# A two-layer hybrid transformer on one core: the norm's shift moves from a row addition to feature columns where transposes leave PSUM, modulation starts two pairs later, the last tile is finished by halves

## The chip, the cores and the metric

The kernel runs on one core of a Trainium2 chip. The metric is the device time of one execution in microseconds (us), as the median of several runs; less is better. A core has TensorE for matrix products and transposes (PE in the profile; PEld is its loading of weights), VectorE (DVE), ScalarE (ACT), GpSimd (POOL) and SyncE (SP), whose queue issues all data transfers of this kernel. Each engine takes its instructions in the order of its own queue. Data is computed on in SBUF, 128 partitions wide; products arrive in PSUM; the inputs and large intermediates lie in device memory.

## The reference

All is in float32: 1024 tokens, 1024 features, two layers. A condition vector gives each layer six rows of 1024 numbers, the modulation: shift, scale and gate for the mixer, shift, scale and gate for the MLP.

```
cond = silu(c)
for l in range(2):
    mod = (cond @ w_ada[l] + b_ada[l])[:, None, :]
    sh_m, sc_m, g_m, sh_f, sc_f, g_f = jnp.split(mod, 6, axis=-1)
    h = _rmsnorm(x, norm_g[l, 0]) * (1.0 + sc_m) + sh_m
    y = _hybrid_mixer(h, ...)        # attention, latent attention, state space model, output projection
    x = x + g_m * _rmsnorm(y, norm_g[l, 1])
    h = _rmsnorm(x, norm_g[l, 2]) * (1.0 + sc_f) + sh_f
    y = jnp.square(jax.nn.relu(h @ w_up[l])) @ w_down[l]
    x = x + g_f * _rmsnorm(y, norm_g[l, 3])
```

The change concerns the lines that make `h`: a norm over the features of a token, a product with a row, and the addition of a shift row.

## The kernel before, in words

**Tiles.** The tokens are eight tiles of 128, the features eight blocks of 128. The norm works token by token, so tokens lie on partitions and features along the row. The products that read `h` want features on partitions. So each normalised tile is transposed on PE into PSUM, block by block, and cut there into two parts, high and low: ACT rounds the value (`nc.scalar.copy`, L611 and L619) and DVE stores what the rounding left (L612 and L620). A product of two such numbers is three matmuls (`mm3`, L192 to L194).

**The norm** (`norm`, L595): ACT squares a tile and sums along the row (L599), `rstd` makes the reciprocal root with one ACT and four DVE instructions (L183 to L187), DVE multiplies by the root and the scale row in one pass (L600), and POOL adds the shift row (L601). Both rows lie in SBUF as 128 equal copies of 1024 numbers, loaded by `mod_load` (L591). In the last two tiles of the layer border the addition is made by DVE (`NVEC`, L1473).

**Where norms run.** Three places use them:

- At the end of each mixer, `renorm` (L1271) takes tiles 0 to 3 beside the output projection of tiles 6 and 7 (L1313), and transposes each by `transp8` with `wide=True` (one PSUM tile of 1024).
- Tiles 4 to 7 follow as `late` while the MLP's first products already run (`mlp_up`, L329 to L333). The up projection uses a scheme that saves products: for each pair `i` of feature blocks, `plain(i)` needs only tiles 0 to 3, and `sums(i)` needs sums and differences of tiles 0 to 3 with 4 to 7. `transp_late` (L201) makes these operands: POOL adds high and low part of tile t-4 (L208), PE transposes tile t, and four differences (L217) are each cut in high and low (L230, L231). Six `plain` stages lead (`LEAD`). Weights come as 512 or 1024 KB loads (L265), POOL forms their sums (L273 to L279), and ACT and DVE cut them.
- At the border of the layers, the last group of the down projection calls `finish(t)` per token tile (L1460). It adds the tile's result to the residual (`Net.finish`, L622: square L628, multiplication L629, addition on POOL L630, store L631), normalises tile t-1 for the next layer, and transposes tile t-3 by narrow steps of four blocks. Tiles 4 to 7 are transposed in `late_norm`, beside the next layer's first projections.

**Modulation.** The rows of the next stages are computed beside the MLP by `mod_stream`, in chunks of 128 columns (`mod_chunk`): a step loads a chunk's weights, bias and gain; the next runs eight multiply-adds on DVE (L540); the third sums over partitions with two small PE products (L551 and L553, both within `bank_t`), adds or multiplies, and stores 128 numbers. In layer 0 there are 56 chunks: two steps after each of 16 pairs in `mlp_up`, the others in `mlp_down`, one after a token tile. In layer 1 there is nothing left to do.

**Order and memory.** The program is written in one order; `TileContext(nc, schedule_with_timeline_sim=True)` sets the order of each engine's queue from a simulated timeline, with the program's order as priority. Row tiles, weights and intermediates share one arena of 17856 words a partition (`Arena`); a block that is given back is used again, and the new user waits for the old one's last reader.

## Time and profile before

| | |
|---|---|
| median of 3 runs | 2843.18 us (2840.31 to 2851.27) |
| the profiled execution | 2845.56 us, its span 2843.7 us |
| mean granted clock of TensorE | 0.955 |
| DMA | 313.10 MB, 110 GB/s on average |

The span goes from the first to the last instruction. A row of the profile names the line of the program, the engine, the operation, what it writes and reads, and its shape; "x24: 1276/1285/3091" is a count with the least, median and greatest duration in ns. In a timeline, a row is start (us), duration, engine, line, operation, and in brackets how long the engine was idle before it and what ended that. In a table of waits, a row is who waited for whom, us in total, times, and the longest. `arena_f` is the arena, `split` the space for high and low parts, `bank_...` a PSUM tile. Where the page breaks the span into 40 slices, the granted clock of PE is:

```
PEclk9899989899989999999989998899998999999999
```

### The profile page before, as it was taken

To read this page: it belongs to the slowest core of one execution; us is meant where nothing else is said; L and a number is where in the kernel's file an instruction comes from. 1 tells how busy PE (TensorE), PEld (TensorE's weight loads), DVE (VectorE), ACT (ScalarE), POOL (GpSimd) and SP (SyncE) were. 2 spreads that over 40 slices of the span, in tenths; PEclk is the share of its full clock that TensorE was granted. 3 is DMA by queue.
4 is the path that set the end of the run, shared out by engine and by line. 5 is a ranking of instruction groups with operands and counts; after the bars stand their busy time and mean duration, and the time that the engine had idled before them with its cause. 6 is when DMAs were issued, how large, how long until landed. Compare 5 with 4: busy or idle time off the path is not lost.

```text
span 2843.7 us, 34676 instructions
## 1 busy us (share of the span) xinstructions
PE 2642.4 (93%) x12530; PEld 2063.0 (73%) x12530; DVE 1734.4 (61%) x3163; ACT 1109.0 (39%) x2129; POOL 641.2 (23%) x533
## 2 busy tenths in 40 slices
PE   5799999898879999999979999989987999999997
PEld 4677776676657777777768777767766888778886
DVE  7767666644878787565463575765458555533435
ACT  5243444544534455121142443445445455621112
POOL 1441233210433320000042113342014433000002
PEclk9899989899989999999989998899998999999999
DMA  6441212313355457443140131132134333531303
GB/s 224 115 136 53 91 51 83 97 62 110 115 162 163 152 175 239 131 149 119 67 138 32 56 93 47 57 112 87 52 111 123 129 112 115 190 125 67 119 30 119
DMA packets 265551, 313.10 MB, mean 110 GB/s; under 512 B 25570, under 2 KB 209060, under 8 KB 265380
## 3 DMA queue, kind: packets, MB, share of 16 engines
q1 hardware_dynamic: 265380, 310.88, 34.1%
q8 instruction: 99, 1.62, 0.2%
q14 instruction: 72, 0.59, 0.1%
HBM read 244.41 MB, written 66.43 MB: 109 GB/s over the span
## 4 chain that ended last, share of the span: by engine, by line
PE 66%; DVE 8%; DMA 6%; issue 4%; ACT 3%; POOL 2%; SPq 0%; POOLq 0%; DVEq 0%; ACTq 0%
PE bank_b L192 10%; PE bank_b L194 10%; PE bank_b L193 10%; PE bank_s L192 8%; PE bank_s L193 8%; PE bank_s L194 8%; PE bank_a L843 2%; PE bank_s L896 2%; DVE split L231 2%; PE bank_t L856 2%; DMA arena_f<-in_w_up 1%; DVE arena_f L540 1%; DMA d_r<-arena_f 1%; PE bank_a L872 1%; PE bank_b L1189 1%
## 5 line engine op out<-in xcount | busy, mean ns | idle before, releaser
L192 PE MATMUL bank_b<-split 128*128 128x512 f32 (+2 forms) x1824 | 727.4, 399 | 36.1 <-ACT split L230 15.5
L193 PE MATMUL bank_b<-split 128*128 128x512 f32 (+2 forms) x1824 | 709.9, 389 | 2.3 <-DVE split L612 1.9
L194 PE MATMUL bank_b<-split 128*128 128x512 f32 (+2 forms) x1824 | 708.1, 389 | 1.6 <-DVE split L231 1.2
L230 ACT CAST split<-arena_f 128x512 fp32r<-128x512 f32 (+1 forms) x384 | 282.9, 761 | 693.5 <-PE bank_s L193 432.9
L192 PE MATMUL bank_s<-split 128*128 128x512 f32 (+2 forms) x1152 | 454.3, 397 | 17.4 <-ACT arena_f L376 7.0
L193 PE MATMUL bank_s<-split 128*128 128x512 f32 (+2 forms) x1152 | 450.4, 391 | 9.2 <-DVE split L231 6.5
L194 PE MATMUL bank_s<-split 128*128 128x512 f32 (+2 forms) x1152 | 447.6, 389 | 0.0
L192 PEld LDWEIGHTS bank_b<-split 128*128 128x128 f32 x1824 | 353.1, 194 | 119.3 <-issue 17.4
L231 DVE TENSOR_TENSOR split<-arena_f,split 128x512 fp32r<-128x512 f32 (+1 forms) x384 | 358.1, 950 | 97.7 <-ACT split L230 96.1
L194 PEld LDWEIGHTS bank_b<-split 128*128 128x128 f32 x1824 | 352.7, 193 | 70.9 <-issue 2.5
L193 PEld LDWEIGHTS bank_b<-split 128*128 128x128 f32 x1824 | 353.8, 194 | 67.2 <-issue 4.7
L378 DVE TENSOR_TENSOR arena_f<-arena_f,bank_s 128x1024 f32<-128x1024 f32 x128 | 156.1, 1219 | 263.1 <-PE bank_s L194 263.1
L192 PEld LDWEIGHTS bank_s<-split 128*128 128x128 f32 (+1 forms) x1152 | 217.7, 190 | 73.2 <-ACT arena_f L376 8.8
L193 PEld LDWEIGHTS bank_s<-split 128*128 128x128 f32 (+1 forms) x1152 | 218.8, 190 | 56.6 <-DVE split L231 9.0
L194 PEld LDWEIGHTS bank_s<-split 128*128 128x128 f32 (+1 forms) x1152 | 218.6, 190 | 43.8 <-issue 1.0
L831 ACT ACTIVATE arena_f<-bank_s,nm 128x128 f32<-128x128 f32 (+3 forms) x192 | 141.9, 741 | 182.7 <-DVE nm L830 151.3
L830 DVE TENSOR_REDUCE nm<-bank_s 128x1 f32<-128x128 f32 (+3 forms) x192 | 142.0, 752 | 113.4 <-PE bank_s L898 58.0
L540 DVE SCALAR_TENSOR_TENSOR arena_f<-arena_f,cond 128x128 f32<-128x128 f32 x448 | 164.5, 396 | 56.4 <-DMA arena_f<-in_b_ada 27.2
L630 POOL TENSOR_TENSOR arena_f<-arena_f 128x1024 f32<-128x1024 f32 x16 | 39.5, 2470 | 479.6 <-DVE arena_f L629 473.7
L246 ACT ACTIVATE arena_f<-arena_f 128x512 f32<-128x512 f32 x128 | 80.8, 632 | 137.0 <-DVE arena_f L320 61.6
L896 PE MATMUL bank_s<-split 32*128 32x512 f32 (+3 forms) x576 | 120.8, 384 | 12.3 <-ACT arena_f L831 10.0
L859 ACT COPY arena_f<-bank_t 128x512 f32<-128x512 f32 (+1 forms) x160 | 86.8, 542 | 105.6 <-PE bank_t L856 91.8
(276 smaller groups left out, 3266.3 us busy)
## 6 DMA issues: line engine op xcount, KB each, us to landing
arena_f<-in_w_ada SPq DMA_DIRECT2D x80, 512.0 KB
d_r<-arena_f SPq DMA_DIRECT2D x128, 256.0 KB
arena_f<-in_w_up SPq DMA_DIRECT2D x32, 1024.0 KB
arena_f<-d_r SPq DMA_DIRECT2D x64, 512.0 KB
arena_f<-in_w_down SPq DMA_DIRECT2D x64, 512.0 KB
arena_f<-d_x SPq DMA_DIRECT2D x36, 512.0 KB
d_x<-arena_f SPq DMA_DIRECT2D x24, 512.0 KB
arena_f<-in_w_in SPq DMA_DIRECT2D x20, 512.0 KB
```

Source lines behind the costliest of these rows:

```text
L192: mm(out, wh, xh, start=start, stop=False)
L193: mm(out, wh, xl, start=False, stop=False)
L194: mm(out, wl, xh, start=False, stop=stop)
L230: self.nc.scalar.copy(hi, src)
L231: (eng or self.nc.vector).tensor_sub(lo, src, f32(hi))
L246: nc.scalar.activation(t, t, AF.Relu)
L378: nc.vector.tensor_add(y[t], y[t], ps)
L540: nc.vector.scalar_tensor_tensor(acc, in0=w[:, k], scalar=self.cond[:, k:k + 1], in1=acc, op0=ALU.mult, op1=ALU.add)
L830: nc.vector.tensor_reduce(nm, S[:, 0:n], axis=AX.X, op=ALU.max, negate=True)
L831: nc.scalar.activation(p[:, 0:n], S[:, 0:n], AF.Exp, bias=nm, accum_out=ls)
L859: nc.scalar.copy(held, ps[:, 0:w])
L896: nc.tensor.matmul(S[mp][:, c0:c1], Q[rw, a, tok], K[rw, b, c0:c1], start=a == b, stop=a == 1 and c1 < n)
```

## The change

The shift is no longer added as a row. `mod_cols` loads it as eight columns, one number per feature, 8 words a partition instead of 1024: element (p, k) comes from address 128 k + p. `norm` ends with the multiplication. `cut_cols` adds the shift while the transposed tile is read from PSUM, feature block by feature block: ACT makes the high part with the column as bias, DVE the low part as (value + column) - high, so a wide tile takes eight instructions on each engine in place of one. In `transp_late` the first two differences take the column in four pieces each, and the high and low part of blocks 4 to 7 are cut by `cut_cols`. The late tiles' operands on POOL (L208) stay.

The modulation of `mlp_up` begins after the third pair (28 steps there in place of 32), and four more steps run in the last but one group of `mlp_down`.

The last token tile of each layer's MLP is finished by halves of 512 features: DVE adds the first half of the product as soon as it is complete, ACT squares the two halves apart, a small DVE instruction adds the two sums, and the multiplication, the addition of the residual (by DVE, not POOL) and the store are made for each half.

At the border the two loaded vectors are given back after the last transposition, not before the first.

```diff
--- before.py
+++ after.py
@@ -29,7 +29,6 @@
 OFF = 0, 0, 0.1, 2
 OUTS = (), (0, 1), (2, 3), (4, 5)
 WOW = 16
-NVEC = 6
 GROUPS = [2] + [4] * 6 + [2, 4]
 LEAD = 6
 C_Q, C_K, C_V, C_CQ, C_CKV, C_KR, C_Z, C_XBC, C_DT = 0, 256, 512, 768, 1024, 1152, 1184, 1696, 2464
@@ -198,7 +197,7 @@
 
         return [self.slot(2 * n, 2, 4, 512) for n in range(4)]
 
-    def transp_late(self, x, hT, t):
+    def transp_late(self, x, hT, t, shift):
 
         nc, F = self.nc, self.F
         T = self.sums()
@@ -211,17 +210,22 @@
             nc.tensor.transpose(ps[:, k * P:k * P + P], x[:, k * P:k * P + P], self.ident)
         pv = ps.rearrange("p (n k q) -> p n k q", n=2, q=P)
 
-        def put(n, a, c):
+        def put(n, a, c, b=None):
 
             e = F.get(4, P)
-            nc.vector.tensor_sub(e, a, c)
+            if b is None:
+                nc.vector.tensor_sub(e, a, c)
+            else:
+                for k in range(4):
+                    nc.vector.scalar_tensor_tensor(e[:, k], in0=a[:, k], scalar=b[:, k:k + 1], in1=c[:, k],
+                                                   op0=ALU.add, op1=ALU.subtract)
             self.split(e, *(T[n][:, m, :, sl] for m in range(2)))
             return e
 
-        e1 = put(0, pv[:, 0], b[0])
-        e2 = put(1, pv[:, 1], e1)
+        e1 = put(0, pv[:, 0], b[0], shift[:, 0:4])
+        e2 = put(1, pv[:, 1], e1, shift[:, 4:8])
+        self.cut_cols(pv[:, 1], shift[:, 4:8], *(h[:, 4:8, tok] for h in hT))
         e3 = put(2, e2, b[0])
-        self.split(pv[:, 1], *(h[:, 4:8, tok] for h in hT))
         e4 = put(3, b[1], e2)
         F.put(e1, e2, e3, e4, *b)
 
@@ -335,8 +339,9 @@
             if i >= LEAD:
                 plain(i)
             sums(i)
-            next(bg, None)
-            next(bg, None)
+            if i > 1:
+                next(bg, None)
+                next(bg, None)
 
     def mlp_down(self, l, y, bg, finish):
 
@@ -367,14 +372,17 @@
             for t in range(NT):
                 tok = slice(t * P, t * P + P)
                 ps = self.bank2()
+                tip = last and t == NT - 1
                 for dh in range(2):
                     dd = slice(dh * 512, dh * 512 + 512)
                     for n, ((_, r), (_, wd)) in enumerate(rw):
                         self.mm3(ps[:, dd], r[:, 0, tok], r[:, 1, tok], wd[:, 0, dd], wd[:, 1, dd], n == 0, n == size - 1)
+                    if tip:
+                        nc.vector.tensor_add(y[t][:, dd], y[t][:, dd], ps[:, dd])
                 if g == 0:
                     y.append(F.get(D, top=True))
                     nc.scalar.copy(y[t], ps)
-                else:
+                elif not tip:
                     nc.vector.tensor_add(y[t], y[t], ps)
                 if last:
                     finish(t)
@@ -591,16 +599,29 @@
         self.nc.sync.dma_start(t, self.d_mod[l, sec:sec + 1].to_broadcast([P, D]))
         return t
 
-
-    def norm(self, x, a, b, xn, eng=None):
+    def mod_cols(self, l, sec):
+
+        t = self.F.get(KD)
+        self.nc.sync.dma_start(t, self.d_mod[l, sec].rearrange("(k p) -> p k", p=P))
+        return t
+
+
+    def norm(self, x, a, xn):
 
         nc = self.nc
         ss = self.sm(1, "nss")
         nc.scalar.activation(xn, x, AF.Square, accum_out=ss)
         nc.vector.scalar_tensor_tensor(xn, in0=x, scalar=self.rstd(ss), in1=a, op0=ALU.mult, op1=ALU.mult)
-        (eng or nc.gpsimd).tensor_add(xn, xn, b)
-
-    def transp8(self, x, hi, lo, t, wide=False):
+
+    def cut_cols(self, ps, b, hi, lo):
+
+        nc = self.nc
+        for k in range(ps.shape[1]):
+            nc.scalar.activation(hi[:, k], ps[:, k], AF.Identity, bias=b[:, k:k + 1])
+            nc.vector.scalar_tensor_tensor(lo[:, k], in0=ps[:, k], scalar=b[:, k:k + 1], in1=f32(hi[:, k]),
+                                           op0=ALU.add, op1=ALU.subtract)
+
+    def transp8(self, x, hi, lo, t, wide=False, b=None):
         nc = self.nc
         sl = slice(t * P, t * P + P)
         if wide:
@@ -608,6 +629,9 @@
             for k in range(KD):
                 nc.tensor.transpose(ps[:, k * P:k * P + P], x[:, k * P:k * P + P], self.ident)
             pv = ps.rearrange("p (k q) -> p k q", q=P)
+            if b is not None:
+                self.cut_cols(pv, b, hi[:, :, sl], lo[:, :, sl])
+                return
             nc.scalar.copy(hi[:, :, sl], pv)
             nc.vector.tensor_sub(lo[:, :, sl], pv, f32(hi[:, :, sl]))
             return
@@ -616,8 +640,7 @@
             for k in range(4):
                 nc.tensor.transpose(ps[:, k * P:k * P + P], x[:, (k0 + k) * P:(k0 + k) * P + P], self.ident)
             pv = ps.rearrange("p (k q) -> p k q", q=P)
-            nc.scalar.copy(hi[:, k0:k0 + 4, sl], pv)
-            nc.vector.tensor_sub(lo[:, k0:k0 + 4, sl], pv, f32(hi[:, k0:k0 + 4, sl]))
+            self.cut_cols(pv, b[:, k0:k0 + 4], hi[:, k0:k0 + 4, sl], lo[:, k0:k0 + 4, sl])
 
     def finish(self, y, src, g, dst, t, x, u, junk):
 
@@ -625,6 +648,21 @@
         tok = slice(t * P, t * P + P)
         nc.sync.dma_start(x, src[tok])
         ss = self.sm(1, "fss")
+        if t == NT - 1:
+
+            s2 = self.sm(2, "fss")
+            for h in range(2):
+                dd = slice(h * 512, h * 512 + 512)
+                nc.scalar.activation(junk[:, h * 4:h * 4 + 4], y[:, dd].rearrange("p (k q) -> p k q", q=P), AF.Square,
+                                     accum_out=s2[:, h:h + 1])
+            nc.vector.tensor_scalar(ss, s2[:, 0:1], s2[:, 1:2], None, op0=ALU.add)
+            rs = self.rstd(ss)
+            for h in range(2):
+                dd = slice(h * 512, h * 512 + 512)
+                nc.vector.scalar_tensor_tensor(u[:, dd], in0=y[:, dd], scalar=rs, in1=g[:, dd], op0=ALU.mult, op1=ALU.mult)
+                nc.vector.tensor_add(x[:, dd], x[:, dd], u[:, dd])
+                nc.sync.dma_start(dst[tok, dd], x[:, dd])
+            return
         nc.scalar.activation(junk, y.rearrange("p (k q) -> p k q", q=P), AF.Square, accum_out=ss)
         nc.vector.scalar_tensor_tensor(u, in0=y, scalar=self.rstd(ss), in1=g, op0=ALU.mult, op1=ALU.mult)
         nc.gpsimd.tensor_add(x, x, u)
@@ -1277,13 +1315,13 @@
         else:
             x = F.get(D)
             self.nc.sync.dma_start(x, src[t * P:t * P + P])
-        self.norm(x, *nxt, u)
+        self.norm(x, nxt[0], u)
         F.put(x)
         yield 1.0
         if t < 4:
-            self.transp8(u, hT[0], hT[1], t, True)
+            self.transp8(u, hT[0], hT[1], t, True, nxt[1])
         else:
-            self.transp_late(u, hT, t)
+            self.transp_late(u, hT, t, nxt[1])
         F.put(u)
         yield 1.0
 
@@ -1308,7 +1346,7 @@
             self.weave((1.0, self.chain(*(out(t, cTs[t % 2]) for t in OUTS[i])), OFF[i]),
                        ((4 + i * 16 + 20) / 11.5 / len(OUTS[i]), self.until(m, i)))
         self.drain(m)
-        nxt = self.mod_load(l, 4), self.mod_load(l, 3)
+        nxt = self.mod_load(l, 4), self.mod_cols(l, 3)
         kept = {}
         self.weave((26, self.chain(out(6, own(6), kept), out(7, own(7), kept))),
                    (9, self.chain(*(self.renorm(t, dst, nxt, hT) for t in range(4)))))
@@ -1462,15 +1500,15 @@
                     tail["g"] = self.mod_load(l, 5)
                     tail["x"] = [F.get(D) for _ in range(3)]
                     if more:
-                        tail["nxt"] = (self.mod_load(l + 1, 1), self.mod_load(l + 1, 0))
+                        tail["nxt"] = (self.mod_load(l + 1, 1), self.mod_cols(l + 1, 0))
                         tail["w"] = list(self.stage_w(I["w_in"][l + 1], self.qk_cols(0), 2))
                 if more and t == NT - 1:
                     tail["w0"] = self.load_w(tail["w"], 2)
                 if more and 2 < t < 7:
-                    self.transp8(y[t - 3], hT[0], hT[1], t - 3)
+                    self.transp8(y[t - 3], hT[0], hT[1], t - 3, False, tail["nxt"][1])
                     F.put(y[t - 3])
                 if more and 0 < t <= NT:
-                    self.norm(tail["x"][(t - 1) % 3], *tail["nxt"], y[t - 1], nc.vector if t > NVEC else nc.gpsimd)
+                    self.norm(tail["x"][(t - 1) % 3], tail["nxt"][0], y[t - 1])
                 if t < NT:
                     self.finish(y[t], self.d_x[2 * l], tail["g"], o, t, tail["x"][t % 3], y[t],
                                 hT[0][:, :, t * P:t * P + P])
@@ -1487,11 +1525,11 @@
                 F.put(tail["g"])
                 if more:
                     finish(NT)
-                    F.put(*tail["nxt"])
                     for t in range(4, NT):
-                        self.transp8(y[t], hT[0], hT[1], t, True)
+                        self.transp8(y[t], hT[0], hT[1], t, True, tail["nxt"][1])
                         F.put(y[t])
                         yield
+                    F.put(*tail["nxt"])
                 else:
                     F.put(*y)
                 F.put(*tail["x"])
```

## Prediction

> **What bounds the kernel now.** I read the page first, then three tables by stage, then the waits of PE in the same stages. The page gives the span and the busiest engine:
>
> ```profile
> span 2843.7 us, 34676 instructions
> PE 2642.4 (93%) x12530; PEld 2063.0 (73%) x12530; DVE 1734.4 (61%) x3163; ACT 1109.0 (39%) x2129; POOL 641.2 (23%) x533
> ```
>
> PE is busy for all but 201 us, so only an edit that lets PE start earlier counts. The change touches four places: the late tiles beside the first products of the MLP in layer 0 and in layer 1, the border between the layers, and the very end. The first three (columns: stretch, its length, busy time of each engine, granted clock, DMA share, GB/s):
>
> ```profile
> 720.00:830.00 110.00, 85.01 (x362) 66.50 (x363) 90.79 (x163) 50.59 (x92) 42.39 (x27) 0.89 0.45 136
> 2120.00:2230.00 110.00, 92.85 (x405) 74.06 (x404) 85.28 (x129) 56.52 (x102) 53.62 (x32) 0.92 0.39 122
> 1465.00:1540.00 75.00, 53.64 (x273) 45.27 (x272) 43.27 (x75) 26.25 (x47) 30.28 (x12) 0.80 0.25 80
> ```
>
> PE lacks 25.0 us in the first, 17.2 in the second, 21.4 in the third: a third of all its idle time in a tenth of the span. What it waited for there, in the same order (two rows for the first, one for the second, two for the third):
>
> ```profile
> PE bank_t L551 <- DVE arena_f L540: 12.7, 1, 12.7
> PE bank_t L551 <- DVE arena_f L559: 3.0, 2, 2.6
> PE bank_b L192 <- ACT split L230: 11.4, 3, 6.7
> PE bank_t L617 <- POOL arena_f L601: 14.1, 1, 14.1
> PE bank_s L609 <- DVE arena_f L601: 6.0, 1, 6.0
> ```
>
> L551 and L540 belong to the modulation, L601 is the addition of the shift row, L230 cuts weights into high and low part. So two of the three edits name the releaser of a long wait of PE.
>
> **Border of the layers: the shift leaves the norm.** Two tiles running, on POOL and on DVE:
>
> ```profile
> 1490.93 3.36 POOL L601 TENSOR_TENSOR arena_f<-arena_f 128x1024 f32<-128x1024 f32 x1 [4.03 <-DVE arena_f L600]
> 1494.26 2.39 POOL L630 TENSOR_TENSOR arena_f<-arena_f 128x1024 f32<-128x1024 f32 x1
> 1500.48 3.38 POOL L601 TENSOR_TENSOR arena_f<-arena_f 128x1024 f32<-128x1024 f32 x1 [3.84 <-DVE arena_f L600]
> ```
>
> ```profile
> 1499.11 1.29 DVE L600 SCALAR_TENSOR_TENSOR arena_f<-arena_f,rstd_y 128x1024 f32<-128x1024 f32 x1
> 1500.32 1.28 DVE L629 SCALAR_TENSOR_TENSOR arena_f<-arena_f,rstd_y 128x1024 f32<-128x1024 f32 x1
> ```
>
> This is a ring with a period of 9.55 us (1490.93 to 1500.48). L630, the residual of tile t, stands on POOL's queue behind L601 of tile t-1; the norm of tile t waits for L630; its L600 stands in front of L629 of tile t+1. Without L601 the round is L630's start to L600's (1494.26 to 1499.11, 4.85), L600 and L629 at 1.21 from start to start, so 7.3 us: 2.25 less for each of tiles 4 to 7, and tile 7 also loses its own L601 on DVE. About 10 us of advance stands against PE's second wait of 6.0. The first wait loses tile 3's own addition, 3.3, and pays about 0.5 for small pieces (priced below): 2.8. That brings PE to tile 7 2.8 earlier, so the ring needs 8.8 in all, and has 10. I take 2.8 + 6.0 = 8.8. PE's clock in this stretch is 0.80: 53.64 x 0.20 = 10.7 us lost behind its two long waits; with one of them gone I credit 2, well under half. Border: **10.8**, from 5 (only tile 3 and one round) to 16 (the first wait shrinks too, because the stretched DVE pieces around it get shorter).
>
> **Modulation two pairs later.** In layer 0, tile 7's operands and the first weights of the sums share DVE with modulation steps, and POOL waits for them too:
>
> ```profile
> 782.43 0.39 PE L194 MATMUL bank_b<-split 128*128 128x512 f32 x1
> 800.17 0.80 PE L192 MATMUL bank_b<-split 128*128 128x512 f32 x1
> ```
>
> ```profile
> 782.62 2.78 DVE L540 SCALAR_TENSOR_TENSOR arena_f<-arena_f,cond 128x128 f32<-128x128 f32 x3 [2.32 <-DMA arena_f<-in_w_ada]
> 792.63 2.81 DVE L540 SCALAR_TENSOR_TENSOR arena_f<-arena_f,cond 128x128 f32<-128x128 f32 x8
> ```
>
> ```profile
> 796.25 1.26 POOL L273 TENSOR_TENSOR arena_f<-arena_f 128x512 f32<-128x512 f32 x1 [11.10 <-DVE arena_f L540]
> ```
>
> Between its last plain product and its first product on sums PE waits and runs modulation products, nothing else: 17.7 us from start to start. Without modulation there, tile 7's four differences follow its transposes directly, without L540 in front of them and between them, and L273 doesn't wait for the block that L540 gives back. Read directly, PE would resume some 2.7 us after 782.8, and 14.7 would be won. Layer 1 is the other bound: it has no modulation in this place, and PE still lacks 17.2 us there, for weights whose loads come late; the difference of the two stretches is 7.8. I take **10**, nearer to layer 1, since its stretch is the same code without the work that moves.
>
> A step that moves takes along its loads of weights, bias and gain and its store on SP, eight L540 on DVE, a memset on POOL, two products on PE. Four of them land behind the last ones of this stage, in the product of the down projection:
>
> ```profile
> L540 DVE SCALAR_TENSOR_TENSOR arena_f<-arena_f,cond x200: 329/347/354, 1099.8 to 1336.6; 128x128 f32<-128x128 f32 x100
> 1340.00:1400.00 60.00, 58.52 (x256) 46.80 (x256) 20.81 (x20) 6.00 (x6) 0.00 (x0) 1.00 0.15 45
> ```
>
> 4 x 8 x 0.347 = 11 us of DVE go where it has 39 of 60 idle, and DMA is at 0.15. I put that at 0; if these steps slid into the last eight tiles, which PE passes in half the time, it would cost up to 4.
>
> **Small pieces where transposes leave PSUM.** Eight additions of one feature block each replace one instruction of 1024. Neither engine shows just this form; the nearest rows are the 128x128 forms with a per-row operand on ACT and from PSUM on DVE:
>
> ```profile
> L831 ACT ACTIVATE arena_f<-bank_s,nm 128x128 f32<-128x128 f32 x24 | 8.7, 368 | 17.4 <-DVE nm L830 16.8 <-PE bank_b L1207 0.6
> L611 ACT CAST split<-bank_s 128x1024 fp32r<-128x1024 f32 x28 | 28.3, 1015 | 22.2 <-PE bank_s L609 22.0
> L874 DVE TENSOR_TENSOR arena_f<-bank_a,ml_rl 128x128 f32<-128x128 f32 x32 | 9.2, 288 | 36.6 <-PE bank_a L872 24.2 <-ACT arena_f L1255 7.7 <-ACT arena_f L831 3.5
> L612 DVE TENSOR_TENSOR split<-bank_s,split 128x1024 fp32r<-128x1024 f32 x28 | 34.1, 1222 | 17.1 <-ACT split L611 16.7
> L217 DVE TENSOR_TENSOR arena_f<-bank_s,arena_f 128x512 f32<-128x512 f32 x16 | 11.0, 686 | 1.3 <-POOL arena_f L208 1.0
> ```
>
> A wide tile costs DVE 8 x 0.288 - 1.222 = 1.08 more and ACT 8 x 0.368 - 1.015 = 1.93 more; ACT is busy 51 of 110 us in the late stretch, which covers it. The latency from transposes to the last piece is at most 8 x 0.368 + 0.288 = 3.2 instead of 2.24. A late tile has eight pieces for two L217 (+0.93) and four for one more 128x512 form (4 x 0.288 - 0.686 = +0.47): 1.40 on DVE. A narrow tile pays 8 x 0.288 - 2 x 0.686 = 0.93. Twelve wide, eight late and four narrow tiles: 13.0 + 11.2 + 3.7 = 28 us of DVE in all. [...] What comes back:
>
> ```profile
> L601 POOL TENSOR_TENSOR arena_f<-arena_f 128x1024 f32<-128x1024 f32 x22 | 62.3, 2836 | 166.7 <-DVE arena_f L600 148.2 <-ACT arena_f L859 12.5 <-issue 3.2
> L600 DVE SCALAR_TENSOR_TENSOR arena_f<-arena_f,rstd_y 128x1024 f32<-128x1024 f32 x24 | 38.8, 1625 | 1.7 <-DMA arena_f<-d_mod 1.2
> L600 DVE SCALAR_TENSOR_TENSOR arena_f<-arena_f,rstd_y x24: 1276/1285/3091, 697.4 to 2180.7; 128x1024 f32<-128x1024 f32 x24
> L540 DVE SCALAR_TENSOR_TENSOR arena_f<-arena_f,cond x24: 341/352/1234, 776.8 to 795.1; 128x128 f32<-128x128 f32 x24
> ```
>
> Each tile is transposed 2.84 us earlier, less at most 1 for the small pieces. And L600, in itself 1.28, takes up to 3.09 while POOL adds beside it; its mean is 1.62, so 24 x 0.34 = 8 us come back on DVE from this line alone. In layer 0 the late stretch also gives away L540, of which it had 24 ahead of 800 (8 us by the median), against 4 x 1.40. Each DVE piece waits for ACT's piece of the same block, which runs one ahead; behind it on DVE stand the next tile's norm and the low parts of weights, and PE behind those, which is why DVE's load is a rival below. In the two late stretches I therefore take a small gain, **1.5 each**, from -3 to +3: what is late next there are the loads of w_up, which no edit hurries, except that the shift takes 8 words for each row instead of 1024 and leaves a block for one more load.
>
> The shift's new load, in the place of the second L591, has 1024 pieces of four bytes:
>
> ```profile
> q1 hardware_dynamic: 265380, 310.88, 34.1%
> 689.91 1.58 SPq L591 DMA_DIRECT2D arena_f<-d_mod  x2
> 703.24 1.01 ACT L611 CAST split<-bank_s 128x1024 fp32r<-128x1024 f32 x1 [0.38 <-PE bank_s L609]
> ```
>
> 0.341 x 16 x 2843.7 / 265380 makes 58 ns a packet, so 64 on each of 16 engines are an estimated 3.7 us; its first reader, which takes the place of this L611, comes 12 us behind the issue. I cost it at 0, and up to 3 if a packet of four bytes takes several times as long.
>
> **Last tile by halves.**
>
> ```profile
> 2832.68 1.22 DVE L378 TENSOR_TENSOR arena_f<-arena_f,bank_s 128x1024 f32<-128x1024 f32 x1 [0.63 <-PE bank_s L194]
> 2833.93 1.06 ACT L628 ACTIVATE split<-arena_f 128x1024 fp32r<-128x1024 f32 x1 [3.96 <-DVE arena_f L378]
> 2835.11 0.29 ACT L183 ACTIVATE rstd_y<-fss,eps 128x1 f32<-128x1 f32 x1
> 2836.20 1.28 DVE L629 SCALAR_TENSOR_TENSOR arena_f<-arena_f,rstd_y 128x1024 f32<-128x1024 f32 x1
> 2837.56 2.34 POOL L630 TENSOR_TENSOR arena_f<-arena_f 128x1024 f32<-128x1024 f32 x1 [3.03 <-DVE arena_f L629]
> ```
>
> From L378 to the end of L630 are 7.2 us. After: half the addition (0.69), half the square (the whole took 2833.93 to 2835.11 with its readout; half 0.8), one small sum (0.2), the same 1.1 from L183 to L629, and four half instructions on DVE at 0.62 from start to start (2.5): 5.3. The first half's store is under way by then. **2.3**, from 1.5 to 3.
>
> Sum: 10.8 + 10 + 3 + 2.3 = 26.1 us. The profiled execution took 2845.56 (span and 1.9 around it), so 2819.5; it stood 2.4 above the median of the runs shown, 2843.18, so **2817**.
>
> **Rivals.** *Weights take the place of the wait.* L230 with 11.4 us in layer 1 speaks for it, that layer 0's loads are issued by the same queue too. Then the modulation gives 7.8, the small pieces cost 1.4 x 4 in each late stretch, the border gives 8.8 and the end 2.3: 7.7 in all, 2835.5. *The queues don't follow the program.* The order on each engine comes from a simulated schedule; L551 stands on PE's queue ahead of the sums' products that precede it in the program. If the steps are pulled forward again, the 10 and the two 1.5 fall away: 13 us, 2830. Against it: two pairs are 144 products, 33 us of PE's work at the 58.52 us for 256 above. *DVE becomes the bound.* If POOL's additions were hidden anyway and the 28 us of small pieces lay on the path, less the 8 given back and 2.3 at the end, the time would be 2861. This decides from the point where DVE's busy time in the late stretch comes near its length; it is 91 and 85 of 110 now, and each addition of L601 has PE or DVE waiting behind it at the border, which speaks against.
>
> **How the numbers follow.** About 0.5%, 14 us, can be told from no change. Forecast 0.66, weights 0.16, queues 0.08, DVE 0.10. The forecast's own range is 2802 (border 16, modulation 14.7, late stretches 6, end 3, clock 1) to 2829. The two middle rivals fall within 0.5% (0.24). The range reaches to 2837 to take these in, and leaves out the slower rival and half of what lies around its ends.
>
> **What would show it.** After: no wait of PE on L601's successor of more than a few us past tile 3 at the border, and POOL's L630 some 7 us apart; the gap before the first product on sums in layer 0 under 10 us, with no modulation product in it; the last store's issue about 5 us behind the last L378 half. I am wrong if that gap stays at 17, if PE waits for the small pieces of L611's and L612's successors by more than 10 us in all, or if the waits for L230 grow by what the modulation gave up.

## The result, and the profile after

The changed kernel takes 2820.14 us (median of 4 runs, 2814.24 to 2823.98) against 2846.68 for the kernel before beside it. The ratio is 0.9906, 95% interval 0.9877 to 0.9936: faster, by more than the 0.5% that can be told from no change. Measured again later beside other kernels it was 0.9931 (0.9906 to 0.9956). The forecast, 2817.0 of 2843.18, is a ratio of 0.9908.

The page of the profiled execution after (2822.46 us):

```profile
span 2820.4 us, 34988 instructions
PE 2621.0 (93%) x12530; PEld 2048.1 (73%) x12530; DVE 1747.9 (62%) x3351; ACT 1134.2 (40%) x2265; POOL 576.7 (20%) x509
```

PE does the same 12530 products in 23.3 us less. It lacks 199.4 us of the span, against 201.3: PE waits hardly less, its products became shorter (2642.4 to 2621.0 busy). The granted clock, 0.955 and now 0.958, explains a part of that: the clock lost over the span (its length times one minus the clock) falls from about 128 to 118 us. So the first view says already that the mechanism is not quite the one forecast. The tables by stage, moved to where the same work lies now:

```profile
720.00:830.00 110.00, 92.83 (x403) 74.62 (x404) 92.75 (x196) 59.69 (x126) 37.64 (x27) 0.94 0.39 124
2100.00:2210.00 110.00, 89.32 (x387) 71.40 (x386) 87.47 (x183) 61.52 (x132) 37.84 (x25) 0.89 0.33 106
1450.00:1525.00 75.00, 55.45 (x318) 48.55 (x317) 51.33 (x127) 37.77 (x97) 19.82 (x8) 0.86 0.25 81
```

The late stretch of layer 0 lacks 17.2 us in place of 25.0, that of layer 1 20.7 in place of 17.2, the border 19.6 in place of 21.4, at a clock of 0.86 instead of 0.80. Lines have moved: L192 to L194 are now L191 to L193, L600 is L614, L630 is L668, L265 is L269, L230 and L231 are L234 and L235, and the pieces are L620 (ACT) and L621 (DVE).

**The gap before the sums.** PE's rows in layer 0:

```profile
785.13 0.39 PE L193 MATMUL bank_b<-split 128*128 128x512 f32 x1
788.12 0.50 PE L191 MATMUL bank_b<-split 128*128 128x512 f32 x1 [2.60 <-ACT split L234]
```

From the last plain product to the first on sums are 3.0 us where there were 17.7, and no modulation product stands between. But PE's waits from 690 to 830 us show what is late instead:

```profile
PE bank_b L191 <- ACT split L234: 15.1, 4, 10.4
```

Before, the weights (then L230) cost 4.1 us there. The long one is followed back in three timelines (PE, ACT, SP) and in the table of SP's waits:

```profile
771.14 0.80 PE L191 MATMUL bank_b<-split 128*128 128x512 f32 x1 [10.43 <-ACT split L234]
```

```profile
770.47 1.14 ACT L234 CAST split<-arena_f 128x512 fp32r<-128x512 f32 x2 [1.53 <-DMA arena_f<-in_w_up]
```

```profile
755.12 0.38 SPq L269 DMA_DIRECT2D arena_f<-in_w_up  x1
...
766.41 11.19 SPq L269 DMA_DIRECT2D arena_f<-in_w_up  x3
```

```profile
SPq L269 <- DVE arena_f L217: 16.8, 2, 14.3
SPq L269 <- DVE arena_f L220: 7.9, 1, 7.9
```

SP sends no load of up-projection weights between 755.12 and 766.41. The weights that PE waits for came with the load at 766.41, which ACT cuts from 770.47 on. After a store at 758.36 SP waits 7.9 us for a block of the arena that DVE still holds for the late tiles. The table names L220, the pieces of their first two differences; in time the end fits the cut L235 just ahead of that piece as well. The longer wait of 14.3 us, for L217, the last difference of tile 4, ends at 740.31 and held up an earlier load, sent at 740.38.

**The border.** PE, DVE and POOL there:

```profile
1458.74 1.03 PE L641 MATMUL bank_t<-ident,arena_f 128*128 128x128 f32 x8
1472.57 1.94 PE L630 MATMUL bank_s<-ident,arena_f 128*128 128x128 f32 x8 [12.79 <-DVE arena_f L614]
...
1481.76 1.97 PE L630 MATMUL bank_s<-ident,arena_f 128*128 128x128 f32 x8 [5.72 <-DVE arena_f L614]
```

```profile
1459.53 3.00 DVE L694 TENSOR_TENSOR split<-arena_f,split 128x1024 fp32r<-128x1024 f32 x1
...
1463.06 5.81 DVE L694 TENSOR_TENSOR split<-arena_f,split 128x1024 fp32r<-128x1024 f32 x3
...
1471.15 1.27 DVE L614 SCALAR_TENSOR_TENSOR arena_f<-arena_f,rstd_y 128x1024 f32<-128x1024 f32 x1
```

```profile
1459.04 2.42 POOL L694 TENSOR_TENSOR split<-arena_f,split 128x848 fp32r<-128x848 f32 x1 [6.14 <-ACT split L693]
...
1473.96 2.36 POOL L668 TENSOR_TENSOR arena_f<-arena_f 128x1024 f32<-128x1024 f32 x1 [6.24 <-DVE arena_f L667]
1483.24 2.37 POOL L668 TENSOR_TENSOR arena_f<-arena_f 128x1024 f32<-128x1024 f32 x1 [6.92 <-DVE arena_f L667]
```

Two waits of 12.8 and 5.7 us stand where 14.1 and 6.0 stood. The norm that PE waits for starts at 1471.15; ahead of it DVE cuts the next layer's weights (L694), stretched beside POOL, which cuts other weights (3.00 us for the first of 128x1024, against 1.21 for this form in the kernel with the columns alone). POOL's additions are 9.28 us apart, hardly less than the 9.55 before.

**The end.** From the last product's second half on:

```profile
2811.91 0.69 DVE L381 TENSOR_TENSOR arena_f<-arena_f,bank_s 128x512 f32<-128x512 f32 x1 [1.15 <-PE bank_s L193]
...
2816.05 1.29 DVE L663 TENSOR_TENSOR arena_f<-arena_f 128x512 f32<-128x512 f32 x2
2816.76 0.94 SPq L664 DMA_DIRECT2D out_x<-arena_f  x2
```

The last addition ends 5.4 us behind that start, against 7.2, and the last store's issue 5.8; the span ends 8.5 behind it, against 11.0.

### The profile page after: what moved, and what is told of

It is laid out like the page before. It is cut to its first block, busy times and chain, and to the rows that moved or that the text cites. A ratio compares the mean times of both kernels' runs of the same rounds, so it can differ in the third digit from the quotient of the medians.

```text
span 2820.4 us, 34988 instructions
## 1 busy us (share of the span) xinstructions
PE 2621.0 (93%) x12530; PEld 2048.1 (73%) x12530; DVE 1747.9 (62%) x3351; ACT 1134.2 (40%) x2265; POOL 576.7 (20%) x509
## 5 line engine op out<-in xcount | busy, mean ns | idle before, releaser
L191 PE MATMUL bank_b<-split 128*128 128x512 f32 (+2 forms) x1824 | 722.9, 397 | 47.1 <-ACT split L234 28.1
L192 PE MATMUL bank_b<-split 128*128 128x512 f32 (+2 forms) x1824 | 707.5, 388 | 0.2 <-DVE split L694 0.2
L193 PE MATMUL bank_b<-split 128*128 128x512 f32 (+2 forms) x1824 | 704.8, 388 | 1.2 <-DVE split L636 1.2
L234 ACT CAST split<-arena_f 128x512 fp32r<-128x512 f32 (+1 forms) x384 | 281.8, 761 | 630.9 <-PE bank_s L192 385.9
L191 PE MATMUL bank_s<-split 128*128 128x512 f32 (+2 forms) x1152 | 454.1, 397 | 17.9 <-ACT split L1061 4.7
L192 PE MATMUL bank_s<-split 128*128 128x512 f32 (+2 forms) x1152 | 450.8, 391 | 9.6 <-DVE split L235 6.7
L193 PE MATMUL bank_s<-split 128*128 128x512 f32 (+2 forms) x1152 | 448.2, 389 | 0.0
L191 PEld LDWEIGHTS bank_b<-split 128*128 128x128 f32 x1824 | 352.5, 193 | 126.9 <-ACT split L234 32.2
L235 DVE TENSOR_TENSOR split<-arena_f,split 128x512 fp32r<-128x512 f32 (+1 forms) x384 | 355.2, 941 | 89.7 <-ACT split L234 88.2
L193 PEld LDWEIGHTS bank_b<-split 128*128 128x128 f32 x1824 | 350.7, 192 | 68.4 <-issue 3.1
L192 PEld LDWEIGHTS bank_b<-split 128*128 128x128 f32 x1824 | 352.4, 193 | 63.8 <-issue 3.9
L191 PEld LDWEIGHTS bank_s<-split 128*128 128x128 f32 (+1 forms) x1152 | 218.1, 190 | 73.5 <-issue 5.8
L192 PEld LDWEIGHTS bank_s<-split 128*128 128x128 f32 (+1 forms) x1152 | 218.9, 190 | 56.8 <-DVE split L235 9.0
L193 PEld LDWEIGHTS bank_s<-split 128*128 128x128 f32 (+1 forms) x1152 | 218.9, 190 | 44.3 <-issue 0.8
L548 DVE SCALAR_TENSOR_TENSOR arena_f<-arena_f,cond 128x128 f32<-128x128 f32 x448 | 155.9, 376 | 50.5 <-DMA arena_f<-in_w_ada 20.7
L668 POOL TENSOR_TENSOR arena_f<-arena_f 128x1024 f32<-128x1024 f32 x14 | 34.5, 2461 | 460.9 <-DVE arena_f L667 453.9
L881 PE MATMUL bank_a<-arena_f 128*64 128x256 f32 (+1 forms) x640 | 108.3, 399 | 19.2 <-ACT arena_f L897 15.0
```

Of the source, the lines that this page charges most:

```text
L191: mm(out, wh, xh, start=start, stop=False)
L192: mm(out, wh, xl, start=False, stop=False)
L193: mm(out, wl, xh, start=False, stop=stop)
L234: self.nc.scalar.copy(hi, src)
L235: (eng or self.nc.vector).tensor_sub(lo, src, f32(hi))
L548: nc.vector.scalar_tensor_tensor(acc, in0=w[:, k], scalar=self.cond[:, k:k + 1], in1=acc, op0=ALU.mult, op1=ALU.add)
```

## The experiments

Single runs of one kernel differ by up to 35.9 us (2834.89 to 2870.75, the kernel before), mostly with the granted clock (over its 89 runs the correlation is -0.86). The changed kernel and one of the variants below have the same order of instructions up to the border, and still took 738.5, 739.7 and 757.1 us to the first result of the MLP. So two more quantities stand beside the ratios. The *clock-weighted time* of a run is its time multiplied by its mean granted clock, what it would take at full clock if all of it followed the clock; it is given as a mean over the runs with its standard error. The *lost clock* is the rest. The kernel before: 2851.5 us in the mean of 89 runs, clock 0.9519, so 2714.4 ± 0.5 weighted and 137 lost. The changed kernel (both measurements, 10 runs): 2825.6, clock 0.9559, 2700.9 ± 1.6 and 125. Of 25.9 us, 13.5 are weighted time and 12.4 are clock.

The weighting takes off too much, though. Among the 89 runs of the kernel before, a clock lower by 0.01 goes with 21.0 ± 1.3 us more time, where the weighting takes off 30, so of two runs of one kernel the one at the lower clock gets the lower weighted time. Where the mean clocks of two kernels differ, the difference *at equal clock* is given too: each mean moved along that slope to 0.9519, the clock of the kernel before. At equal clock the changed kernel takes 17.6 ± 1.4 us less.

Stages are measured between marks in one profile each: up projection from its first copied result (L305) to the first of the down projection (L376); border from the first narrow transpose (L617) to the next layer's first copy of 424 columns (L750).

| us | before | changed | again | delay alone | columns alone | all but delay | no shift |
|---|---|---|---|---|---|---|---|
| up projection, layer 0 | 360.3 | 348.5 | 348.1 | 355.4 | 364.3 | 364.7 | 344.6 |
| border | 106.8 | 101.6 | 101.1 | 110.3 | 100.0 | 109.7 | 99.3 |
| up projection, layer 1 | 332.8 | 331.7 | 330.7 | 332.1 | 334.1 | 329.7 | 331.9 |

The marks don't enclose quite the same work in each kernel, since the order on PE differs: layer 0's up projection has 1440 PE instructions before, 1423 in the changed kernel and 1418 with the delay alone; the border has 474, 476, and 499 in all but delay, so that its 109.7 can't be compared. Up and down projection of layer 0 together (2925 before, 2915 after) are the safer measure: 707.4 us before, 697.0 and 698.3 in the changed kernel, 704.7 with the delay alone.

**The modulation's delay alone**, in the kernel before:

```diff
-            next(bg, None)
-            next(bg, None)
+            if i > 1:
+                next(bg, None)
+                next(bg, None)
```

> The kernel before with one part of the change: modulation in the MLP's up projection begins two pairs later. The forecast: 10 us less than before (7.8 to 14.7), all of it between the first up-projection result of layer 0 and the start of the down projection; the wait of PE for L540 near 782 us is gone, layer 1 unchanged. The rival with the weights: 8 us at most, since PE waits there for weights (a longer wait for L230) instead. The rival with the queues: within 2 us of before.

Ratio 1.0000 (0.9973 to 1.0027): no difference in time. Weighted 2704.1 ± 1.0, so 10.3 less than before; lost clock 149, 12 more. At equal clock it is 7.1 ± 1.3 less. Layer 0's up projection is 4.9 us shorter, but together with the down projection only 2.7. PE's waits from 700 to 830 us:

```profile
PE bank_t L552 <- DVE arena_f L541: 9.7, 1, 9.7
PE bank_b L192 <- ACT split L230: 8.3, 2, 4.2
```

The wait for the modulation (L541 here) is shorter, not gone, and the weights cost 8.3 in place of 4.1. The gain is there when the clock is allowed for, and the clock took it back. Where the clock was lost can't be put down to the edit: in the profile most of the difference lies in the two mixers, and PE's instructions of the first stand in the same order as before. Those of the second don't, though the edit leaves its lines alone: the schedule orders them anew.

**The columns alone** (`mod_cols`, `cut_cols` and their calls; modulation and last tile as before):

> The kernel before with the shift as feature columns alone; modulation and last tile as before. The forecast: 13.8 us less than before, 10.8 of it at the border of the layers and 1.5 in each late stretch. From the two traces so far I expect less at the border (5 us, since the wait that is left there lasts 12.8 us) and a part of the 7.7 us that the up projection of layer 1 gained: 10 to 13 us in all, and the 7.6 us that layer 1's mixer lost are there too if they come from the columns. The rival with VectorE as the bound: no gain or a loss, since 28 us of small pieces then lie on the path.

Ratio 1.0010 (0.9988 to 1.0031); weighted 2712.5 ± 1.0, 1.9 less than before. The border is 6.8 us shorter, layer 0's up projection 4 longer. What was expected of layer 1 is not seen in the stages: its up projection is 1.3 us longer than before, and its mixer, between the border and that, took 588.6 us before, 589.6 and 588.4 in the changed kernel, and 593.5 here. POOL's additions of the residual at the border (L649 here), and PE's waits from 1430 to 1550:

```profile
1484.58 2.35 POOL L649 TENSOR_TENSOR arena_f<-arena_f 128x1024 f32<-128x1024 f32 x1 [1.16 <-DVE arena_f L648]
1492.79 2.36 POOL L649 TENSOR_TENSOR arena_f<-arena_f 128x1024 f32<-128x1024 f32 x1 [5.87 <-DVE arena_f L648]
1500.53 2.40 POOL L649 TENSOR_TENSOR arena_f<-arena_f 128x1024 f32<-128x1024 f32 x1 [5.38 <-DVE arena_f L648]
1507.96 2.40 POOL L649 TENSOR_TENSOR arena_f<-arena_f 128x1024 f32<-128x1024 f32 x1 [5.03 <-DVE arena_f L648]
```

```profile
PE bank_t L637 <- DVE split L617: 11.5, 2, 10.8
PE bank_s L626 <- DVE arena_f L610: 2.8, 1, 2.8
```

Here the ring did shorten, to 8.2, 7.7 and 7.4 us, and the second wait to 2.8. The first, 10.8, is for a PSUM bank that pieces of tile 2 (L617 here) still read. In layer 0's late stretch PE waits 10.6 us for weights as in the changed kernel: the wait belongs to the columns.

**The halves alone** (in `mlp_down` and `finish`; both layers):

> The kernel before with the last token tile of each layer finished by halves alone. The forecast: 2.3 us less, all behind the last product of the kernel; from the two traces 2.5 us less there. At the border tile 7 is also finished by halves: at most 1 us either way. A theory that makes this part worth nothing: the last store's landing sets the end and starts no earlier.

Ratio 1.0006 (0.9986 to 1.0026); weighted 2714.6 ± 1.4, as before. The tail from the last L378 half is as long as in the changed kernel. At the border one wait of 2.8 for the first half of tile 7's addition is new. It can't be told from nothing.

**All but the delay:**

```diff
-            if i > 1:
-                next(bg, None)
-                next(bg, None)
+            next(bg, None)
+            next(bg, None)
```

> The changed kernel with modulation back at its old place, columns and halves kept. If the parts add up, it is 10 us slower than the changed kernel and about 16 us less than before by the forecast (12 to 14 by the traces so far). If the parts depend on one another (the columns' pieces and the modulation's steps share VectorE in layer 0's late stretch), it is slower than that sum: more than 12 us behind the changed kernel.

Ratio 0.9977 (0.9959 to 0.9994); weighted 2711.7 ± 1.5. The delay is worth 10.8 ± 2.2 weighted us on top of the other parts, as much as alone. So in weighted time the parts add up: 10.3 + 1.9 - 0.2 = 12.0, and all together bring 13.5. In plain time they don't: each alone brings nothing, all together 26. At equal clock they don't either: alone 7.1 + 0.5 - 1.5 = 6.1, all together 17.6, and the delay is worth 14.2 ± 1.7 beside the other parts, twice as much as alone. Whether the parts help one another therefore hangs on how the clock is allowed for, and stays open.

**The changed kernel once more**, no edit:

> The changed kernel once more, on one chip with the three kernels below. If its gain is one of the whole and not of the day, the ratio lies again near 0.9906 (26 us). If the parts, each worth nothing alone and 0.2% without the delay, are the truth, it lies near 0.998 (6 us).

0.9931 (0.9906 to 0.9956), weighted 2699.8 ± 2.0. The gain is one of the whole.

**Halves not at the border:**

```diff
-                tip = last and t == NT - 1
+                tip = last and t == NT - 1 and l + 1 == DEPTH
```

(and in `finish` alike)

> The changed kernel, with the halves only where the kernel ends; at the border of the layers tile 7 is finished whole, as before. My theory: at the border the halves hurt, since their pieces on VectorE stand among the cuts and norms that PE waits for: the waits on the norm (12.8 and 5.7 us in the changed kernel) fall to about the 10.8 and 2.8 of the kernel with the columns alone, and the time is 3 to 5 us less than the changed kernel. The rival: the order of the queue does it, not the halves; then within 2 us of the changed kernel.

0.9919 (0.9891 to 0.9948), weighted 2698.8 ± 1.4: the changed kernel within its error. The two waits at the border are 14.5 and 5.7 us. My theory falls: the halves cost nothing there that can be told.

**Weights one pair ahead:**

```diff
-            st = F.get(KD, n)
-            dma(st, w_up[:, :, i * 2 * P:i * 2 * P + n])
+            st = loaded.pop((i, sums), None) or load(i, sums)
+            if not sums:
+                key = (i + 1, False) if not sums and i + 1 < LEAD else (0 if not sums else i + 1, True)
+                loaded[key] = load(*key)
```

(`load` holds the two lines taken out)

> The changed kernel, with each 512 KB load of up-projection weights of the six leading pairs issued one pair earlier, so that it takes another block of the arena than those of tile 4's differences. My theory: PE's wait of 10.4 us in layer 0's late stretch (and of 8.2 in layer 1's) is one for weights whose load waits 14.3 us for the last difference of tile 4 (L217), so both fall below 4 us and the time falls by 8 to 14 us. The rival with VectorE as the bound: the weights come earlier and their cutting still waits for VectorE, so PE waits as long as before for L235 or for tile 7's differences, and the time stays within 3 us.

0.9953 (0.9932 to 0.9974), weighted 2707.4 ± 1.4: 6.5 worse than the changed kernel. The wait did fall, to 5.1 us at the longest where less than 4 was expected, and others came. PE in layer 0's up projection (738 to 1100 us):

```profile
PE bank_b L191 <- DVE arena_f L330: 7.8, 4, 2.8
PE bank_b L191 <- ACT split L234: 6.9, 2, 5.1
```

L330 here adds a product on sums to what DVE holds; PE now waits for DVE to empty its banks while modulation runs beside it. That the late load makes the long wait is confirmed, the gain is not: in layer 0 the next limit stands right behind. Layer 1's up projection took 323.3 us.

**The freed block taken back:**

```diff
-        t = self.F.get(KD)
-        self.nc.sync.dma_start(t, ...)
+        t = self.F.get(D)
+        self.nc.sync.dma_start(t[:, 0:KD], ...)
```

> The changed kernel, with the columns' 8 words in a block of 1024, so that the arena is handed out as in the kernel before. It separates the arena's layout from the pieces. If the freed block is worth something (the prediction said so: room for one more load), it is 2 to 6 us slower than the changed kernel; if the layout it brought is what makes the weights late (10.4 us), it is 4 to 10 us faster; if only the pieces count, within 2 us.

0.9894 (0.9873 to 0.9914), weighted 2699.7 ± 2.2. The weighted time is that of the changed kernel; the plain time is not told apart from it either, since the intervals overlap. The freed block is worth nothing that can be told. PE's waits from 690 to 830 us are others, though:

```profile
PE bank_t L559 <- DVE arena_f L548: 7.8, 1, 7.8
PE bank_b L191 <- ACT split L234: 5.6, 2, 3.0
```

With all the pieces in place, but the arena handed out as before, the long wait for weights is gone, and a wait for the modulation (L548) is back in its stead. So the layout that the freed block brought does make the weights late; in sum that costs nothing that can be told, since another wait takes its place.

**Pieces apart:**

```diff
         for k in range(ps.shape[1]):
             nc.scalar.activation(hi[:, k], ps[:, k], AF.Identity, bias=b[:, k:k + 1])
+        for k in range(ps.shape[1]):
             nc.vector.scalar_tensor_tensor(lo[:, k], ...)
```

> The changed kernel, with the order of the pieces in a tile altered: ScalarE's pieces of a tile all first, then VectorE's, where the changed kernel alternates. In the changed kernel each piece on ScalarE but a bank's first waits for VectorE's piece before it (39 us of waits of ScalarE in all), so eight pieces take up to 6.3 us (0.78 for one) where the prediction had 3.2. My theory: these waits hold up what stands behind them on ScalarE, the cutting of weights above all; without them ScalarE's waits for the pieces fall below 5 us, eight pieces take some 4.5 us, PE's waits for weights (L234, 28 us in all) fall by 5 to 10 us and the time by 4 to 10. The rival: PE waits for loads and norms, not for pieces; then within 2 us of the changed kernel.

The changed kernel's groups for the pieces of wide tiles, and the one of ACT in this kernel:

```profile
L620 ACT ACTIVATE split<-bank_s,arena_f 128x128 fp32r<-128x128 f32 x128 | 44.8, 365 | 45.8 <-DVE split L621 31.5 <-PE bank_s L630 14.0
L621 DVE SCALAR_TENSOR_TENSOR split<-bank_s,arena_f,split 128x128 fp32r<-128x128 f32 x128 | 42.6, 345 | 23.2 <-ACT split L620 22.4
```

```profile
L620 ACT ACTIVATE split<-bank_s,arena_f 128x128 fp32r<-128x128 f32 x128 | 35.1, 381 | 19.3 <-PE bank_s L631 19.3
```

ACT's waits for DVE are gone, and the time is no shorter: 0.9948 (0.9932 to 0.9964), weighted 2701.1 ± 1.1, as the changed kernel. PE's wait for weights in layer 0's late stretch was even 16.9 us long. The rival holds: the alternation costs nothing that PE sees.

**Chunks held:**

```diff
+            if hold is not None:
+                nc.scalar.copy(wt[:, 0, k0, 0:1], hold[:, 0:1])
             nc.scalar.copy(wt[:, 0, k0:k0 + step], st)
```

> The changed kernel, with the cutting of the next layer's second and third weight chunk held until tiles 4 and 5 are normalised (a copy of one number a piece makes the wait; all work stays). In the changed kernel the second chunk's cuts take 9 us of VectorE beside GpSimd's cut of the third, ahead of tile 4's norm. My theory: these cuts set PE's wait of 12.8 us at the border, not the shift; it falls to 4 to 8 us, the stretch from the first narrow transposes to the next layer's first scores shrinks by 4 to 9 us. The rival: the ring of GpSimd and VectorE sets the norms; then the wait stays within 2 us, or moves to the second chunk's first product.

PE's rows at the border:

```profile
1475.44 1.97 PE L641 MATMUL bank_t<-ident,arena_f 128*128 128x128 f32 x8 [7.86 <-DVE split L621]
1487.42 1.97 PE L630 MATMUL bank_s<-ident,arena_f 128*128 128x128 f32 x8 [8.26 <-DVE arena_f L614]
```

The first wait falls as expected, by 4.9 us, and the second rises by 2.5; the stretch is 100.5 us, about 1 less than the changed kernel's. 0.9938 (0.9915 to 0.9961), weighted 2702.9 ± 2.5. The weights' cuts are one cause of the first wait; behind them come tile 2's pieces and tile 4's norm, so removing them alone wins nothing.

**No shift, whole cuts:**

```diff
-            if b is not None:
-                self.cut_cols(pv, b, hi[:, :, sl], lo[:, :, sl])
-                return
             nc.scalar.copy(hi[:, :, sl], pv)
             nc.vector.tensor_sub(lo[:, :, sl], pv, f32(hi[:, :, sl]))
```

(and alike in the narrow tiles and in `transp_late`)

> The changed kernel without the shift: no column is added, each transposed tile is cut by one instruction on each engine, or two, as before (so the modulation's shift is left out of the result; its 8 words are still loaded). It prices the pieces: the prediction put 28 us more on VectorE and nothing on the path. If that holds, VectorE is 20 to 28 us less busy and the time is within 3 us of the changed kernel. If the pieces are on the path (the rival with VectorE as the bound), it is 8 to 25 us less.

0.9866 (0.9838 to 0.9894), weighted 2689.4 ± 0.9: 11.5 ± 1.9 less than the changed kernel, and 12.5 ± 1.9 at equal clock. Its engines, and PE's waits from 690 to 830 (one row) and from 1440 to 1560 us (two):

```profile
PE 2637.4 (94%) x12530; PEld 2059.5 (73%) x12530; DVE 1725.3 (61%) x3171; ACT 1109.3 (39%) x2133; POOL 576.3 (20%) x509
```

```profile
PE bank_b L191 <- ACT split L234: 10.5, 3, 8.6
PE bank_t L638 <- DVE arena_f L614: 9.6, 1, 9.6
PE bank_s L630 <- DVE arena_f L614: 2.0, 1, 2.0
```

DVE is 22.6 us and ACT 24.9 less busy, and PE lacks 179.6 us of the span in place of 199.4 and 193.6. The small pieces cost time, about half of what they cost DVE; since ACT's pieces go with DVE's, the run doesn't tell the two engines apart. At the border PE waits 11.6 us in place of 18.5 for the norms. The long wait for weights in layer 0 is still 8.6: most of it isn't the pieces'.

**Ahead in layer 1 alone** (the edit above, with `if l and not sums`):

> The changed kernel, with the loads of the leading pairs' weights one pair earlier in layer 1 alone. With it in both layers the up projection of layer 1 took 323.3 us in place of 331.7 and 330.7, and that of layer 0, where modulation shares VectorE with the sums, 359.3 in place of 348.5 and 348.1. My theory: the early load pays where VectorE has time behind it; so layer 0 is as in the changed kernel (348 us, the wait of 10.4 us stays), layer 1's up projection takes 323 to 326 us, and the time is 5 to 8 us less than the changed kernel, a ratio of 0.988 to 0.991 to before. The rival: what layer 1 gained is given back at its down projection or was a matter of the clock; then the ratio is that of the changed kernel, 0.991 to 0.993.

0.9933 (0.9910 to 0.9957), weighted 2700.0 ± 1.0: as the changed kernel. Layer 1's up projection took 325.3 us as expected, and the rest of the kernel behind it 366.0 where the changed kernel took 361.9 and 361.2. PE's waits from 2400 us on begin with:

```profile
PE bank_s L191 <- ACT arena_f L394: 3.2, 2, 2.1
```

L394 (L384 in the changed kernel, 0.3 us there) is the first copy of the down projection, late on ACT. My theory falls: most of it is given back.

None of the variants that compute the whole is told apart from the changed kernel as better.

## Why the prediction was right, and where only its sum was

**Modulation, 10 us: right in size.** The delay is worth 10.3 ± 1.1 weighted us alone and 10.8 ± 2.2 beside the rest (7.1 and 14.2 at equal clock), and in the changed kernel layer 0's up and down projection together are 10.4 and 9.1 us shorter. With the delay alone they are only 2.7 shorter in its one profile, so there the gain isn't shown to lie where it was forecast. The gap is 3.0 us as asked for, under 10 and without a modulation product. What came late next are the weights, as the rival with that name said: their waits rise from 4.1 to 15.1 in the stretch (by 11.0, where the modulation's gave up 15.7), which took most of the 14.7 that the upper bound held and left the 7.8 of the lower (25.0 to 17.2 idle). The rival's other half, that layer 1 and the pieces hold nothing more, is what its 2835.5 rested on, and the sum went elsewhere. The moved steps cost little that shows: the stretch from the down projection to the border went from 347.1 to 348.5 and 350.2 us, within the 4 allowed.

**Small pieces, a gain of 1.5 in each late stretch: wrong in sign.** The term was a balance: 28 us of DVE "covered" against earlier transposes. By their rows DVE's pieces cost 345 ns, not 288, ACT's 365, as priced from L831. What was to come back came back, 24 x 0.33 = 8 us in the norm's multiplication (1.625 to 1.295 us in the mean):

```profile
L614 DVE SCALAR_TENSOR_TENSOR arena_f<-arena_f,rstd_y 128x1024 f32<-128x1024 f32 x24 | 30.8, 1295 | 1.3 <-DMA arena_f<-d_mod 1.0
```

The pieces, though, are not covered: without them 11.5 us are won. The step that failed is "ACT is busy 51 of 110 us in the late stretch, which covers it": an engine's mean load doesn't say what stands in its queue behind the pieces. Where the 11.5 lie is shown in part. At the border, where I had put 0.5 for the pieces, PE's two waits for norms on DVE are 6.9 us shorter without them; in layer 0's late stretch the waits for weights are 4.6 shorter (15.1 to 10.5). The rest of the long wait there comes with the freed block: it is gone with the pieces but the old layout. So the rival with DVE as the bound was right that the pieces lie on the path, at 11.5 of its 28; that it is DVE's pieces rather than ACT's is argued, not shown. My sign for it, waits of PE for L620 and L621 by more than 10 us, looked at the wrong place: PE waits for weights and norms that stand behind the pieces. Layer 1's late stretch, which was to gain 1.5 too, lacks 3.5 us more than before.

**Border, 10.8: about half, and not as told.** The ring of POOL and DVE was right for the columns alone (7.4 to 8.2 us a tile against 7.3 forecast). In the changed kernel it stays at 9.28; that weights and pieces fill DVE's round there is argued, not shown. So two of the signs that I had named for the border failed: PE still waits 12.8 us past tile 3, and POOL's additions are not some 7 us apart. The step that failed is that the first wait ends with the shift (2.8 less): before it, too, DVE cuts weights there, and with the shift gone it is the cuts, then the pieces' PSUM bank, then the norm that come last. The two waits fell by 1.6 together (20.1 to 18.5); the stage is 5.2 and 5.7 us shorter, the rest of it clock (0.80 to 0.86 in the stretch, PE busy 85.6 to 82.2 us in the stage), for which I had credited 2. One profile says little here: with the delay alone, which leaves the border's lines as they were, the stage took 110.3 in place of 106.8.

**Last tile, 2.3: right by its rows**, 2.5 there (11.0 to 8.5), and too small to be seen alone. The rows of the forecast give 1.9 (7.2 - 5.3), and 1.8 came up to the last addition; the rest is the shorter store.

**The sum.** Columns and halves were to bring 16 and bring about 2 to 3 weighted us; the clock was to bring 2 and brings 12 (8 at equal clock, where 17.6 of the 25.9 remain). The forecast of 26 was met by one right term and by two errors of opposite sign; that they cancel is luck. Of the clock's 12 us, 5 to 7 lie in the two profiles between the first result of layer 0's MLP and the end of the border (by the granted clock in windows of 8 us, 25.6 us lost before, 18.8 and 20.5 after). What gave the rest, and why the delay alone lost 12 where the whole won them, stays open: the first mixer, whose order the change hardly touches, took 738.5 to 757.1 us in profiles of one order, a scatter wider than what is to be explained.

## What to carry to other kernels

Where a row operation is traded for many small pieces, price the pieces by what stands behind them in their engine's queue, not by the engine's mean load: here 22.6 us of VectorE and 24.9 of ScalarE cost 11.5 us of time at 61% and 39% load. A wait that is removed uncovers the next one in the same stretch; follow it before counting (here modulation, then a load that waits for a block, then banks to be emptied). Where runs differ by their clock, compare them at equal clock beside the plain time, or parts that are each worth something look worth nothing; and take the price of the clock from many runs of one kernel (here 21 us per 0.01), since multiplying by the clock took off more than that here (30 us per 0.01).

## What the runs showed of the hardware

*The clock differs between runs of the same instructions.* Single runs of the kernel before went from 2834.89 to 2870.75 us at clocks of 0.957 and 0.948, and by the 89 runs 0.01 of clock goes with 21 us. In the changed kernel eight transposes took 1.94 us after a wait of 12.79 us, against 1.03 of the eight ahead of it; the granted clock was 1.00 from 1448 to 1459.8 us, 0.68 from there to 1466, and 0.50 from 1466 to 1474.6. Why it differs from run to run was not shown. The lost clock is 137 of 2851 us here, 4.8%.

*Readers of one PSUM tile on two engines took turns.* With the pieces interleaved ACT's often waited on a semaphore for DVE's piece ahead of it, though neither writes the tile in PSUM: 31.5 us of ACT's idle time over 128 pieces. It goes when all of ACT's pieces precede DVE's: the 19.3 us of idle time left are waits for PE. The semaphores are part of the program as built; that the chip would need this order is not shown.

*Beside POOL's instructions some of DVE's took longer.* DVE's norm multiplication has a mean of 1.295 us without L601 beside it, and took up to 3.09 with it (three others beside a POOL addition for 1 us or more kept their 1.28); a cut of weights of 128x1024 took 3.00 beside a cut and an addition on POOL, against 1.21 for the same form in the kernel with the columns alone.
